# VectorE's maxima and list operations in the order of the text, and two groups of loads issued with later sets of rows

## The chip, the cores and the metric

One core of a Trainium2 chip runs the kernel. The metric is the time of one execution in microseconds on the device; 2252.41 us is the median of three runs before the change. The engines are TensorE (PE in the profile; PEld is its weight load), VectorE (DVE), ScalarE (ACT), GpSimd (POOL) and SyncE (SP), which only issues transfers here.

## The reference

One layer over 256 latent tokens of width 2048: a norm, one projection, an mLSTM and a differential attention side by side, an output projection, and then PEER, a retrieval of experts. The change lies in PEER:

```python
def peer(h, w_pq, sub_keys, expert_u, expert_v):
    q = (h @ w_pq).reshape(B, T, P_HEADS, 2, P_KEY_DIM // 2)
    s = jnp.einsum('bthpd,hpnd->bthpn', q, sub_keys)
    s1, i1 = lax.top_k(s[..., 0, :], P_TOPK)
    s2, i2 = lax.top_k(s[..., 1, :], P_TOPK)
    ...
    idx = jnp.take_along_axis(cand_i, pos, axis=-1)      # expert i1 * 128 + i2
    g = jax.nn.softmax(top_s, axis=-1)
    ...
        act = gelu(jnp.einsum('td,ted->te', hx, expert_u[ix]))
        return jnp.einsum('te,ted->td', gx * act, expert_v[ix])
```

Each token takes 8 heads x 16 of the 16384 experts; each expert is a row of `expert_u` and a row of `expert_v`, 2048 wide. After it, `x + g2 * peer(...)` and a last norm.

## The kernel before

**First product, for all experts.** The kernel multiplies all of `expert_u` with the 256 tokens: 128 blocks of 128 experts, two to a call of `u_pair` (L1229 to L1244) in the loop over `i1`. A block gives one tile `s` in PSUM (two buffers), from two *pieces*. A piece is taken by `take()`, which stages up to three pieces ahead with `stage()`: a 512 KB load `raw` on SyncE's queue (L118), ScalarE's cast to `hi` (L140), and `lo` = raw − hi (L143) on VectorE, or for every fourth piece on POOL. `raw`, `hi` and `lo` have three buffers each. PE then runs eight matmuls with `hi` (512 columns) and eight with `lo` (256 columns). After two pieces VectorE reduces `s` to `act` (L1244), ScalarE applies Gelu (L1713), and `act` goes to a DRAM array (`ag_dram`).

**Beside it, a plan.** After each piece `pump` steps the generator `plan()` 1.15 to 1.7 times (`pace`). It runs, in this order:

- `retrieve`: which experts each token takes, and the softmax.
- `gate_map(t)`, for both halves of the tokens, in two halves each: one-hot matmuls (`g<-o,o`) write the gate of every expert and token to PSUM, ScalarE copies them to `gates`, and `map_out` (L1266 to L1275) then stores a half map by eight transfers of 512 KB on SyncE's queue, in rows of 256 bytes (L1271). Beside each store VectorE takes a maximum over tokens (`most`, L1272), and at the end it copies `gate_tail`.
- `lists()`: from `most`, which experts are used by which groups of tokens (`use`, `many`, `k1`, `kp`, `k2`, `k3`, `single`, `pairs`); `fill` places each kind of expert by matmuls (`g<-pairs,from_on` is the first) and a scan (L1368); `hots` makes one-hot rows (`h`, `at`; L1432, L1433, L1436) whose matmuls `g<-h,h` give the indices of the gathers.
- `soon()`: the second product for the first nine sets of four blocks of rows of `expert_v`. Rows and gates are gathered by indirect transfers on POOL (L1532). The sets are numbered by `n`; the eight rows of sets 0 and 1 are gathered at the start. `resident()` holds eight loads of 256 KB for the end of the kernel: four of `x1` (L1637) and four of `g2` (L1649). `next(loads, None)` issues one with each row of a set, as long as there are any.

The blocks behind that, `v_item`, multiply the rest of `expert_v`.

**What sets the order.** Each engine runs its instructions in the order of its queue. A scheduler orders them ahead of time by its own estimate of times; `tc.keep_in_program_order(i)` holds `i` behind the instruction that the text issued just before it on that engine. Before the change PE's matmuls (`mp_`), the stores, the loads of this phase and the gathers are held so; VectorE's operations are not, until `soon()` begins (`line`).

Of the kernel before, what the change touches and what calls it, by code (L numbers as in the profile page):

```python
# [26 lines left out]
OP = mybir.AluOpType  # L27
AX = mybir.AxisListType
# [59 lines left out]
def build(tc, a, dump=None):  # L88
# [1176 lines left out]
    def map_out(gates, t, hf_):  # L1265
        rows = ag_dram[P:].rearrange("(i p) t -> p i t", p=P)  # L1266
        at = 2 * t * P + 3 * HT * hf_
        w = slice(at, at + HT)
        for i in range(0, P, 16):
            g, j = gates[i // 64], i % 64  # L1270
            tc.keep_in_program_order(nc.sync.dma_start(rows[:, i:i + 16, w], g[:, j:j + 16, :]))  # L1271
            nc.vector.reduce_max(most[:, 4 * t + 2 * hf_:4 * t + 2 * hf_ + 2, i:i + 16].rearrange("p g i -> p i g"),  # L1272
                                 g[:, j:j + 16, :].rearrange("p i (g c) -> p i g c", g=2), axis=AX.X)
            yield
        nc.vector.tensor_copy(gate_tail[:, :, t * P + hf_ * HT:t * P + (hf_ + 1) * HT], gates[1][:, N_LIST - 64:, :])  # L1275
# [32 lines left out]
    def lists():  # L1308
# [4 lines left out]
        nc.vector.memset(one, 1.0)  # L1313
# [4 lines left out]
        nc.vector.tensor_tensor(from_on, from_on, one, op=OP.subtract)  # L1318
        t0 = ls.tile([P, P], F32, name="t0")
        row = ls.tile([P, 1], F32, name="row")  # L1320
        nc.vector.tensor_tensor(t0, ident, iota, op=OP.mult)
        nc.vector.reduce_sum(row, t0, axis=AX.X)
        nc.vector.tensor_scalar(row, row, 1.0, None, op0=OP.add)
        iota4 = ls.tile([P, P, 4], BF16, name="iota4")
        nc.vector.tensor_copy(iota4, b3(iota, 4))
        column = ls.tile([P, N_LIST], BF16, name="column")
        nc.vector.tensor_scalar(column, iota[:, 0:N_LIST], 1.0, None, op0=OP.add)
        yield
        use = ls.tile([P, 8, N_LIST], F32, name="use")
        nc.vector.tensor_scalar(use, most[:, :, 0:N_LIST], 0.0, None, op0=OP.is_gt)  # L1330
        yield
        many = ls.tile([P, 2, N_LIST], F32, name="many")
        for t in range(2):
            nc.vector.reduce_sum(many[:, t], use[:, 4 * t:4 * t + 4].rearrange("p g i -> p i g"), axis=AX.X)
# [4 lines left out]
        nc.vector.memset(zero, 0.0)  # L1339
        nc.vector.tensor_tensor(k1[:, 0], many[:, 0], many[:, 1], op=OP.add)  # L1340
        nc.vector.tensor_scalar(k1, k1, 1.0, None, op0=OP.is_equal)
        yield
        nc.vector.tensor_scalar(k2, many, 1.0, None, op0=OP.is_equal)
        nc.vector.tensor_tensor(kp[:, 0], k2[:, 0], k2[:, 1], op=OP.mult)
        nc.vector.tensor_scalar(k2, many, 0.0, None, op0=OP.is_gt)
        nc.vector.tensor_tensor(k3[:, 0], k2[:, 0], k2[:, 1], op=OP.mult)
        nc.vector.tensor_tensor(k2, k2, k3.to_broadcast([P, 2, N_LIST]), op=OP.subtract)
# [8 lines left out]
        def fill(kind, size, bases):  # L1356
            n, w = kind.shape[1:]
            pre, tot = (psG.tile([P, 4, P], F32, name="g", tag="g").rearrange("p a b -> p (a b)")[:, 0:n * w].rearrange(
                "p (c i) -> p c i", c=n) for _ in range(2))
            rank = ls.tile([P, 4, N_LIST], F32, name="rank", tag="rank", bufs=2)[:, 0:n, 0:w]  # L1360
            pw = put[:, 0:n, 0:w]
            yield
            yield
            mp_(pre, lhsT=from_on, rhs=kind, start=True, stop=True)
            mp_(tot, lhsT=one, rhs=kind, start=True, stop=True)
            yield
            for c in range(n):
                nc.vector.tensor_tensor_scan(rank[:, c], tot[:, c], zero[:, 0:w], 0.0, op0=OP.add, op1=OP.add)  # L1368
            yield
            nc.vector.tensor_tensor(rank, rank, pre, op=OP.add)  # L1370
            nc.vector.scalar_tensor_tensor(pw, rank, float(size * P), kind, op0=OP.is_lt, op1=OP.mult)
            if n == 4:
                nc.vector.tensor_tensor(half_gone[:, :, 0:w], pw[:, 0:2], pw[:, 2:4], op=OP.add)
                pw2 = half_gone[:, :, 0:w]
            else:
                pw2 = pw
            if n == 1:
                nc.vector.tensor_copy(gone[:, 0:w], pw[:, 0])
            else:
# [10 lines left out]
        nc.vector.tensor_tensor(single, use, k1.to_broadcast([P, 8, N_LIST]), op=OP.mult)  # L1390
        nc.vector.tensor_tensor(use[:, 0:4], use[:, 0:4], kp.to_broadcast([P, 4, N_LIST]), op=OP.mult)
        for d in range(4):
            nc.vector.tensor_tensor(pairs[:, 0:4 - d], use[:, 0:4 - d], use[:, 4 + d:], op=OP.mult)
# [20 lines left out]
        nc.vector.tensor_tensor(over, k3[:, 0], gone, op=OP.subtract)  # L1414
# [3 lines left out]
        nc.vector.reduce_sum(zero, places.rearrange("p c i -> p i c"), axis=AX.X)  # L1418
        nc.vector.tensor_scalar(placei[:, 2], zero, float(NOWHERE), None, op0=OP.add)
        nc.vector.tensor_scalar(placei[:, 1], placei[:, 2], P - 1, None, op0=OP.bitwise_and)  # L1420
        nc.vector.tensor_scalar(placei[:, 0], placei[:, 2], 7, None, op0=OP.logical_shift_right)
        nc.vector.tensor_copy(hl, placei[:, 0:2])
# [3 lines left out]
        def hots(i):  # L1426
            i = min(i, N_LIST - 4)
            w = slice(i, i + 4)
            o1 = ls.tile([P, P, 4], BF16, name="h1", tag="h1", bufs=3)
            o2 = ls.tile([P, 4, 2, N_BLOCKS], BF16, name="h2", tag="h2", bufs=3)  # L1430
            at = ls.tile([P, 4, N_BLOCKS], BF16, name="at", tag="at", bufs=2)
            nc.vector.tensor_tensor(o1, hl[:, 1, w].unsqueeze(1).to_broadcast([P, P, 4]), iota4, op=OP.is_equal)  # L1432
            nc.vector.tensor_tensor(at, b3(hl[:, 0, w], N_BLOCKS),  # L1433
                                    iota[:, 0:N_BLOCKS].unsqueeze(1).to_broadcast([P, 4, N_BLOCKS]), op=OP.is_equal)
            nc.scalar.activation(o2[:, :, 0], at, AF.Copy, scale=row)
            nc.vector.tensor_tensor(o2[:, :, 1], at, b3(column[:, w], N_BLOCKS), op=OP.mult)  # L1436
            return o1, o2
# [214 lines left out]
    def soon():  # L1652
# [24 lines left out]
        for n, item in enumerate(work):  # L1677
# [233 lines left out]
```

## Time and profile before

| | us |
|---|---|
| median of three runs | 2252.41 (2245.99 to 2253.37) |
| the profiled execution | 2240.84 |
| its span | 2239.1 |
| PE busy in it | 2146.8 (96%) |
| VectorE busy in it | 1536.1 (69%) |
| ScalarE busy in it | 1022.1 (46%) |
| POOL busy in it | 784.5 (35%) |

The page of the profile shows one execution; times in it count from the start of the span. The first product with its plan fills about 1200 to 2050 us: the maxima of the maps lie between 1347.7 and 1524 us, the lists run from there to about 1755, `soon()` from about 1755 on. A row of the timeline gives the start, the length, the engine, the line, the operation, output<-inputs and shapes, xcount, and in brackets how long the engine had been idle and what ended it. "SPq" rows are SyncE issuing transfers.

### The profile page before, as it was taken

How to read it: one execution, taken by the hardware profiler on the slowest of the kernel's cores; microseconds unless marked ns; L12 is line 12 of the kernel's file. 1: busy time of each engine (PE TensorE's matmuls, PEld its weight loads, DVE VectorE, ACT ScalarE, POOL GpSimd, SP SyncE). 2: the span in 40 equal slices, each digit the busy share in tenths (PEclk: the TensorE clock that was granted, in tenths of full speed). 3: DMA queues.
4: the chain of work that ended last, by engine and by line, in shares of the span. 5: the costliest groups of instructions: out<-in, count | busy, mean ns of one | idle time of the engine just before them, and what ended most of it. 6: DMA issues, size and time to landing. Idle time of an engine off the chain costs nothing. (4 is left out here: it accounts for less than half of the span.)

```text
span 2239.1 us, 37163 instructions
## 1 busy us (share of the span) xinstructions
PE 2146.8 (96%) x14098; PEld 1860.9 (83%) x14098; DVE 1536.1 (69%) x2781; ACT 1022.1 (46%) x1634; POOL 784.5 (35%) x799
## 2 busy tenths in 40 slices
PE   6999999999999999998999999998999999999996
PEld 3668998999899899987998888897888877786773
DVE  3438794566987786855679967777989644544664
ACT  3222232224465854444444678883446333333552
POOL 2122210225554321000223667781221323416763
PEclk9999999999999999999999999999999999999998
DMA  9958883776654678875556568888665798989995
GB/s 379 368 172 310 317 298 96 272 260 195 166 167 131 191 252 279 284 251 179 183 170 193 187 187 236 227 221 235 210 201 183 296 331 332 356 327 380 413 406 226
DMA packets 235845, 563.63 MB, mean 252 GB/s; under 512 B 85218, under 2 KB 118803, under 8 KB 222096
## 3 DMA queue, kind: packets, MB, share of 16 engines
q1 hardware_dynamic: 155328, 339.34, 46.1%
q0 software_dynamic: 45488, 204.33, 25.2%
q10 hardware_dynamic: 34848, 17.57, 2.7%
q8 instruction: 111, 1.82, 0.3%
q14 instruction: 70, 0.57, 0.1%
HBM read 516.99 MB, written 38.93 MB: 248 GB/s over the span
## 5 line engine op out<-in xcount | busy, mean ns | idle before, releaser
L140 ACT CAST hi<-raw 128x1024 fp32r<-128x1024 f32 x528 | 553.2, 1049 | 849.5 <-PE acc L300 275.3
L143 DVE TENSOR_TENSOR lo<-raw,hi 128x1024 fp32r<-128x1024 f32 x476 | 602.4, 1269 | 376.5 <-ACT hi L140 341.3
L94 PE MATMUL s<-h,hi 128*128 128x512 f32 x2048 | 529.1, 400 | 14.5 <-ACT hi L140 13.7
L94 PEld LDWEIGHTS s<-h,hi 128*128 128x128 f32 x2048 | 369.6, 190 | 93.4 <-ACT hi L140 19.3
L300 PE MATMUL acc<-hL,hi 128*128 128x256 f32 x2048 | 333.5, 284 | 0.0
L94 PEld LDWEIGHTS s<-h,lo 128*128 128x128 f32 x2048 | 280.3, 191 | 30.0 <-DVE lo L143 5.5
L300 PEld LDWEIGHTS acc<-hL,hi 128*128 128x128 f32 x2048 | 292.6, 192 | 1.8 <-ACT kA L677 0.3
L94 PE MATMUL s<-h,lo 128*128 128x256 f32 x2048 | 287.1, 283 | 6.9 <-DVE lo L143 3.8
L143 POOL TENSOR_TENSOR lo<-raw,hi 128x1024 fp32r<-128x1024 f32 x52 | 133.6, 2570 | 305.2 <-ACT hi L140 256.7
L300 PE MATMUL acc<-hL,lo 128*128 128x256 f32 x1024 | 175.7, 284 | 0.9 <-DVE lo L143 0.9
L533 DVE SCALAR_TENSOR_TENSOR raw<-raw,cr 128x1024 f32<-128x1024 f32 x128 | 156.3, 1234 | 21.3 <-DMA raw<-w_mod 17.3
L118 POOL DMA_DIRECT2D raw<-w_mod x128 | 67.9, 530 | 289.9 <-DVE raw L533 276.4
L1261 POOL TENSOR_SCALAR o<-iota,i1T,gT 128x128 f32<-128x128 f32 x128 | 147.5, 1160 | 56.4 <-PE g L94 27.9
L1532 POOL DMA_INDIRECT vraw<-expert_v,idxV x96 | 101.5, 1057 | 167.5 <-PE v L94 83.5
L300 PEld LDWEIGHTS acc<-hL,lo 128*128 128x128 f32 x1024 | 150.0, 192 | 2.2 <-DVE lo L143 1.3
L1532 POOL DMA_INDIRECT ag<-ag_dram,idxG x96 | 109.9, 1145 | 79.7 <-DMA ag_dram<-act 37.4
L1561 DVE TENSOR_TENSOR lo<-vraw,hi 128x1024 fp32r<-128x1024 f32 x68 | 82.9, 1225 | 68.4 <-ACT hi L1559 68.2
L300 PE MATMUL acc<-hC,hi 128*128 128x256 f32 x512 | 124.7, 283 | 0.0
L1244 DVE TENSOR_REDUCE act<-s 128x256 f32<-128x512 f32 x126 | 86.1, 684 | 51.0 <-PE s L94 47.4
L94 PE MATMUL v<-hi,l 128*128 128x512 f32 x416 | 114.5, 397 | 0.1
L1559 ACT CAST hi<-vraw 128x1024 fp32r<-128x1024 f32 x68 | 70.8, 1049 | 79.7 <-PE v L94 62.7
L300 PEld LDWEIGHTS acc<-hC,hi 128*128 128x128 f32 x512 | 98.3, 192 | 0.0
(440 smaller groups left out, 3313.4 us busy)
## 6 DMA issues: line engine op xcount, KB each, us to landing
raw<-expert_u SPq DMA_DIRECT2D x256, 512.0 KB, 4.2
raw<-w_in SPq DMA_DIRECT2D x176, 512.0 KB, 4.5
raw<-w_mod POOLq DMA_DIRECT2D x128, 512.0 KB, 5.5
raw<-w_mod SPq DMA_DIRECT2D x64, 512.0 KB, 8.6
raw<-w_out SPq DMA_DIRECT2D x32, 512.0 KB, 4.3
raw<-w_pq SPq DMA_DIRECT2D x32, 512.0 KB, 3.4
ag_dram<-gates SPq DMA_DIRECT2D x32, 512.0 KB, 6.2
ag_dram<-act ACTq DMA_DIRECT2D x126, 128.0 KB, 4.6
```

Source lines behind the costliest of these rows:

```text
L94: tc.keep_in_program_order(mm(*args, **kw))
L118: d = queue.dma_start(r, src)
L140: nc.scalar.copy(h, r)
L143: (nc.vector if shared[0] else nc.gpsimd).tensor_tensor(l, r, h.bitcast(F32), op=OP.subtract)
L300: mm(acc[c][:, g * T:(g + 1) * T], lhsT=hl[sb][:, k2 * 512 + c * P:k2 * 512 + (c + 1) * P], rhs=rhs(sa, g, k), start=first and k2 == 0 and ...
L533: product = nc.vector.scalar_tensor_tensor(r, r, 1.0, cr, op0=OP.mult, op1=OP.mult, accum_out=part[:, h, i:i + 1])
L1244: line(nc.vector.reduce_sum(act[:, e], ps.rearrange("p s t -> p t s"), axis=AX.X))
L1261: (nc.gpsimd if i % 2 else nc.vector).tensor_scalar(o2[:, i], iota, cols[:, i:i + 1], factor[:, i:i + 1], op0=OP.is_equal, op1=OP.mult)
L1532: tc.keep_in_program_order(nc.gpsimd.indirect_dma_start(out=out, out_offset=None, in_=src, in_offset=bass.IndirectOffsetOnAxis(ap=idx[:, b ...
L1559: nc.scalar.copy(h, raw)
L1561: nc.vector.tensor_tensor(l, raw, h.bitcast(F32), op=OP.subtract)
```

## The change

A wrapper `vector` holds each VectorE operation that goes through it behind the one before it in the text. `map_out` and all of `lists()` use it (about 60 calls; the remaining ones differ in nothing but that name). In `soon()` the loads are issued only for `n > 1`, so `x1` goes with the rows of the third set and `g2` with those of the fourth.

```diff
+    class InOrder:
+        def __getattr__(self, name):
+            f = getattr(nc.vector, name)
+            return lambda *args, **kw: tc.keep_in_program_order(f(*args, **kw))
+
+    vector = InOrder()
...
             tc.keep_in_program_order(nc.sync.dma_start(rows[:, i:i + 16, w], g[:, j:j + 16, :]))
-            nc.vector.reduce_max(most[:, 4 * t + 2 * hf_:4 * t + 2 * hf_ + 2, i:i + 16].rearrange("p g i -> p i g"),
+            vector.reduce_max(most[:, 4 * t + 2 * hf_:4 * t + 2 * hf_ + 2, i:i + 16].rearrange("p g i -> p i g"),
                                  g[:, j:j + 16, :].rearrange("p i (g c) -> p i g c", g=2), axis=AX.X)
             yield
-        nc.vector.tensor_copy(gate_tail[:, :, t * P + hf_ * HT:t * P + (hf_ + 1) * HT], gates[1][:, N_LIST - 64:, :])
+        vector.tensor_copy(gate_tail[:, :, t * P + hf_ * HT:t * P + (hf_ + 1) * HT], gates[1][:, N_LIST - 64:, :])
...
-        nc.vector.tensor_tensor(single, use, k1.to_broadcast([P, 8, N_LIST]), op=OP.mult)
-        nc.vector.tensor_tensor(use[:, 0:4], use[:, 0:4], kp.to_broadcast([P, 4, N_LIST]), op=OP.mult)
+        vector.tensor_tensor(single, use, k1.to_broadcast([P, 8, N_LIST]), op=OP.mult)
+        vector.tensor_tensor(use[:, 0:4], use[:, 0:4], kp.to_broadcast([P, 4, N_LIST]), op=OP.mult)
         for d in range(4):
-            nc.vector.tensor_tensor(pairs[:, 0:4 - d], use[:, 0:4 - d], use[:, 4 + d:], op=OP.mult)
+            vector.tensor_tensor(pairs[:, 0:4 - d], use[:, 0:4 - d], use[:, 4 + d:], op=OP.mult)
...
             for j, b in enumerate(item):
                 new[j] = (stage_rows(*b) if n > 1 else rows.pop(0)), new[j]
-                next(loads, None)
+                if n > 1:
+                    next(loads, None)
                 yield
```

PE's queue is the same before and after. VectorE's queue at the last map, before: `most` are its maxima, `gate_tail` the copy behind them, `act` and `lo` the first product's own work.

```order
L1244 TENSOR_REDUCE act<-s 128x256
L143 TENSOR_TENSOR lo<-raw,hi 128x1024
L1272 TENSOR_REDUCE most<-gates 128x16x2 x8
L1275 COPY gate_tail<-gates 128x2x64
L1244 TENSOR_REDUCE act<-s 128x256
L143 TENSOR_TENSOR lo<-raw,hi 128x1024
L1330 TENSOR_SCALAR use<-most 128x1008
L1334 TENSOR_REDUCE many<-use 128x126 x2
```

And after, from the row behind the copy of the half map before it (L136 is the wrapper, L150 is L143, L1251 is L1244):

```order
L136 TENSOR_REDUCE most<-gates 128x16x2
L1251 TENSOR_REDUCE act<-s 128x256
L136 TENSOR_REDUCE most<-gates 128x16x2
L150 TENSOR_TENSOR lo<-raw,hi 128x1024
L136 TENSOR_REDUCE most<-gates 128x16x2 x2
L1251 TENSOR_REDUCE act<-s 128x256
L150 TENSOR_TENSOR lo<-raw,hi 128x1024
L136 TENSOR_REDUCE most<-gates 128x16x2
L1251 TENSOR_REDUCE act<-s 128x256
L136 COPY gate_tail<-gates 128x2x64
```

The batch of eight is taken apart; `act` and `lo` stand between the maxima. The last three come behind the rows shown, again with a `lo` between.

VectorE's queue where `pairs` is made for the first list matmul, before; the scan of that matmul's result (`rank`, L1368) comes eight rows below the last one shown:

```order
L1344 TENSOR_TENSOR kp<-k_16173 128x126
L1390 TENSOR_TENSOR single<-use,k_16170 128x1008
L1345 TENSOR_SCALAR k_16173<-many 128x252
L1391 TENSOR_TENSOR use<-use,kp 128x504
L1346 TENSOR_TENSOR k_16172<-k_16173 128x126
L1393 TENSOR_TENSOR pairs<-use 128x504
L1347 TENSOR_TENSOR k_16173<-k_16173,k_16172 128x252
```

And after, up to that scan:

```order
L1251 TENSOR_REDUCE act<-s 128x256
L136 TENSOR_TENSOR single<-use,k_16170 128x1008
L136 TENSOR_TENSOR kp<-k_16173 128x126
L136 TENSOR_SCALAR k_16173<-many 128x252
L136 TENSOR_TENSOR use<-use,kp 128x504
L150 TENSOR_TENSOR lo<-raw,hi 128x1024
L136 TENSOR_TENSOR k_16172<-k_16173 128x126
L136 TENSOR_TENSOR pairs<-use 128x504
L136 TENSOR_TENSOR k_16173<-k_16173,k_16172 128x252
L136 SCALAR_TENSOR_TENSOR rank<-g,zero 128x126 x4
```

Before, six operations of `lo` lay between `pairs` and the scan; now none does, and an `act` and a `lo` stand between the first list operations and `pairs`.

SyncE's queue from the end of the last map's stores to the first load of `g2`, before:

```order
L118 DMA raw<-expert_u 128x1024 x81
L1637 DMA x_18691<-x_dram 128x512
L118 DMA raw<-expert_u 128x1024
L1637 DMA x_18692<-x_dram 128x512
L1637 DMA x_18693<-x_dram 128x512
L118 DMA raw<-expert_u 128x1024
L1637 DMA x1m<-x_dram 128x512
L118 DMA raw<-expert_u 128x1024 x4
L1649 DMA g_0_18860<-g_dram 128x512
```

And after:

```order
L118 DMA raw<-expert_u 128x1024 x94
L1644 DMA x_19051<-x_dram 128x512
L118 DMA raw<-expert_u 128x1024
L1644 DMA x_19052<-x_dram 128x512
L1644 DMA x_19053<-x_dram 128x512
L118 DMA raw<-expert_u 128x1024
L1644 DMA x1m<-x_dram 128x512
L118 DMA raw<-expert_u 128x1024 x6
L1656 DMA g_0_19296<-g_dram 128x512
```

The loads of `x1` stand 13 row loads later and those of `g2` 15; nothing else on this queue moves.

More of the change, by code (lines that the diff above doesn't have):

```diff
@@ L1312, in lists @@
         one = ls.tile([P, P], BF16, name="one")
-        nc.vector.memset(one, 1.0)
+        vector.memset(one, 1.0)
         from_on = ls.tile([P, P], BF16, name="from_on")
@@ L1317, in lists @@
                                 channel_multiplier=-1)
-        nc.vector.tensor_tensor(from_on, from_on, one, op=OP.subtract)
+        vector.tensor_tensor(from_on, from_on, one, op=OP.subtract)
         t0 = ls.tile([P, P], F32, name="t0")
         row = ls.tile([P, 1], F32, name="row")
-        nc.vector.tensor_tensor(t0, ident, iota, op=OP.mult)
-        nc.vector.reduce_sum(row, t0, axis=AX.X)
-        nc.vector.tensor_scalar(row, row, 1.0, None, op0=OP.add)
+        vector.tensor_tensor(t0, ident, iota, op=OP.mult)
+        vector.reduce_sum(row, t0, axis=AX.X)
+        vector.tensor_scalar(row, row, 1.0, None, op0=OP.add)
         iota4 = ls.tile([P, P, 4], BF16, name="iota4")
-        nc.vector.tensor_copy(iota4, b3(iota, 4))
+        vector.tensor_copy(iota4, b3(iota, 4))
         column = ls.tile([P, N_LIST], BF16, name="column")
-        nc.vector.tensor_scalar(column, iota[:, 0:N_LIST], 1.0, None, op0=OP.add)
+        vector.tensor_scalar(column, iota[:, 0:N_LIST], 1.0, None, op0=OP.add)
         yield
         use = ls.tile([P, 8, N_LIST], F32, name="use")
-        nc.vector.tensor_scalar(use, most[:, :, 0:N_LIST], 0.0, None, op0=OP.is_gt)
+        vector.tensor_scalar(use, most[:, :, 0:N_LIST], 0.0, None, op0=OP.is_gt)
         yield
@@ L1333, in lists @@
         for t in range(2):
-            nc.vector.reduce_sum(many[:, t], use[:, 4 * t:4 * t + 4].rearrange("p g i -> p i g"), axis=AX.X)
+            vector.reduce_sum(many[:, t], use[:, 4 * t:4 * t + 4].rearrange("p g i -> p i g"), axis=AX.X)
         k1, kp = (ls.tile([P, 1, N_LIST], F32, name=n) for n in ("k1", "kp"))
@@ L1338, in lists @@
         zero = ls.tile([P, N_LIST], F32, name="zero")
-        nc.vector.memset(zero, 0.0)
-        nc.vector.tensor_tensor(k1[:, 0], many[:, 0], many[:, 1], op=OP.add)
-        nc.vector.tensor_scalar(k1, k1, 1.0, None, op0=OP.is_equal)
+        vector.memset(zero, 0.0)
+        vector.tensor_tensor(k1[:, 0], many[:, 0], many[:, 1], op=OP.add)
+        vector.tensor_scalar(k1, k1, 1.0, None, op0=OP.is_equal)
         yield
[L1343 to L1347, printed above, removed]
+        vector.tensor_scalar(k2, many, 1.0, None, op0=OP.is_equal)
+        vector.tensor_tensor(kp[:, 0], k2[:, 0], k2[:, 1], op=OP.mult)
+        vector.tensor_scalar(k2, many, 0.0, None, op0=OP.is_gt)
+        vector.tensor_tensor(k3[:, 0], k2[:, 0], k2[:, 1], op=OP.mult)
+        vector.tensor_tensor(k2, k2, k3.to_broadcast([P, 2, N_LIST]), op=OP.subtract)
         yield
@@ L1367, in fill @@
             for c in range(n):
-                nc.vector.tensor_tensor_scan(rank[:, c], tot[:, c], zero[:, 0:w], 0.0, op0=OP.add, op1=OP.add)
+                vector.tensor_tensor_scan(rank[:, c], tot[:, c], zero[:, 0:w], 0.0, op0=OP.add, op1=OP.add)
             yield
-            nc.vector.tensor_tensor(rank, rank, pre, op=OP.add)
-            nc.vector.scalar_tensor_tensor(pw, rank, float(size * P), kind, op0=OP.is_lt, op1=OP.mult)
+            vector.tensor_tensor(rank, rank, pre, op=OP.add)
+            vector.scalar_tensor_tensor(pw, rank, float(size * P), kind, op0=OP.is_lt, op1=OP.mult)
             if n == 4:
-                nc.vector.tensor_tensor(half_gone[:, :, 0:w], pw[:, 0:2], pw[:, 2:4], op=OP.add)
+                vector.tensor_tensor(half_gone[:, :, 0:w], pw[:, 0:2], pw[:, 2:4], op=OP.add)
                 pw2 = half_gone[:, :, 0:w]
@@ L1377, in fill @@
             if n == 1:
-                nc.vector.tensor_copy(gone[:, 0:w], pw[:, 0])
+                vector.tensor_copy(gone[:, 0:w], pw[:, 0])
             else:
-                nc.vector.tensor_tensor(gone[:, 0:w], pw2[:, 0], pw2[:, 1], op=OP.add)
+                vector.tensor_tensor(gone[:, 0:w], pw2[:, 0], pw2[:, 1], op=OP.add)
             yield
             for c, base in enumerate(bases):
-                nc.vector.scalar_tensor_tensor(rank[:, c], rank[:, c], float(base * P - NOWHERE), pw[:, c],
+                vector.scalar_tensor_tensor(rank[:, c], rank[:, c], float(base * P - NOWHERE), pw[:, c],
                                                op0=OP.add, op1=OP.mult)
-            nc.vector.tensor_tensor(places[:, 0:n, 0:w], places[:, 0:n, 0:w], rank, op=OP.add)
+            vector.tensor_tensor(places[:, 0:n, 0:w], places[:, 0:n, 0:w], rank, op=OP.add)
             yield
@@ L1389, in lists @@
         single = ls.tile([P, 8, N_LIST], BF16, name="single")
-        nc.vector.tensor_tensor(single, use, k1.to_broadcast([P, 8, N_LIST]), op=OP.mult)
-        nc.vector.tensor_tensor(use[:, 0:4], use[:, 0:4], kp.to_broadcast([P, 4, N_LIST]), op=OP.mult)
+        vector.tensor_tensor(single, use, k1.to_broadcast([P, 8, N_LIST]), op=OP.mult)
+        vector.tensor_tensor(use[:, 0:4], use[:, 0:4], kp.to_broadcast([P, 4, N_LIST]), op=OP.mult)
         for d in range(4):
-            nc.vector.tensor_tensor(pairs[:, 0:4 - d], use[:, 0:4 - d], use[:, 4 + d:], op=OP.mult)
+            vector.tensor_tensor(pairs[:, 0:4 - d], use[:, 0:4 - d], use[:, 4 + d:], op=OP.mult)
             if d:
-                nc.vector.tensor_tensor(pairs[:, 4 - d:], use[:, 4 - d:4], use[:, 4:4 + d], op=OP.mult)
+                vector.tensor_tensor(pairs[:, 4 - d:], use[:, 4 - d:4], use[:, 4:4 + d], op=OP.mult)
             yield from fill(pairs, 1, [BASE[PAIR + 4 * d + c] for c in range(4)])
-            nc.vector.tensor_tensor(k3[:, 0], k3[:, 0], gone, op=OP.subtract)
+            vector.tensor_tensor(k3[:, 0], k3[:, 0], gone, op=OP.subtract)
         for t in range(2):
@@ L1413, in lists @@
         over = ls.tile([P, N_LIST], F32, name="over")
-        nc.vector.tensor_tensor(over, k3[:, 0], gone, op=OP.subtract)
+        vector.tensor_tensor(over, k3[:, 0], gone, op=OP.subtract)
         nc.gpsimd.dma_start(over_dram, over)
@@ L1417, in lists @@
         hl = ls.tile([P, 2, N_LIST], BF16, name="hl")
[L1418 to L1422, printed above, removed]
+        vector.reduce_sum(zero, places.rearrange("p c i -> p i c"), axis=AX.X)
+        vector.tensor_scalar(placei[:, 2], zero, float(NOWHERE), None, op0=OP.add)
+        vector.tensor_scalar(placei[:, 1], placei[:, 2], P - 1, None, op0=OP.bitwise_and)
+        vector.tensor_scalar(placei[:, 0], placei[:, 2], 7, None, op0=OP.logical_shift_right)
+        vector.tensor_copy(hl, placei[:, 0:2])
         yield
@@ L1454, in lists @@
         mp_(left, lhsT=ones, rhs=over, start=True, stop=True)
-        nc.vector.reduce_sum(t0[:, 0:1], left, axis=AX.X)
-        nc.vector.tensor_copy(n_over, t0[:, 0:1])
+        vector.reduce_sum(t0[:, 0:1], left, axis=AX.X)
+        vector.tensor_copy(n_over, t0[:, 0:1])
         e, at = (ls.tile([P, N_BLOCKS], F32, name=n) for n in ("e", "e_at"))
-        nc.vector.tensor_copy(at, sums[:, 0])
-        nc.vector.scalar_tensor_tensor(e, sums[:, 1], float(P), at, op0=OP.mult, op1=OP.add)
-        nc.vector.tensor_scalar(at, e, -1.0, float(P - 1), op0=OP.add, op1=OP.max)
+        vector.tensor_copy(at, sums[:, 0])
+        vector.scalar_tensor_tensor(e, sums[:, 1], float(P), at, op0=OP.mult, op1=OP.add)
+        vector.tensor_scalar(at, e, -1.0, float(P - 1), op0=OP.add, op1=OP.max)
         for l in range(BOTH):
             w = slice(BASE[l], BASE[l] + CAPS[l])
-            nc.vector.tensor_scalar(at[:, w], at[:, w], 4.0 if l < 8 else 2.0,
+            vector.tensor_scalar(at[:, w], at[:, w], 4.0 if l < 8 else 2.0,
                                     float(2 * TILES[l][0] + group(l, l // 4) // 2 if l < 8 else TILES[l][0]),
                                     op0=OP.mult, op1=OP.add)
-        nc.vector.tensor_copy(idxG, at)
-        nc.vector.tensor_scalar(e, e, float(-P - 1), 0.0, op0=OP.add, op1=OP.max)
-        nc.vector.tensor_copy(idxV, e)
+        vector.tensor_copy(idxG, at)
+        vector.tensor_scalar(e, e, float(-P - 1), 0.0, op0=OP.add, op1=OP.max)
+        vector.tensor_copy(idxV, e)
         ls.release()
```

16 lines of the change are left out of this document (8 added, 8 removed).

## The prediction

> **What bounds the kernel now.** I read the page first, then tables by stretches of time, then the list of waits, then the instructions one by one where TensorE (PE) stood still.
>
> ```profile
> span 2239.1 us, 37163 instructions
> PE 2146.8 (96%) x14098; PEld 1860.9 (83%) x14098; DVE 1536.1 (69%) x2781; ACT 1022.1 (46%) x1634; POOL 784.5 (35%) x799
> ```
>
> PE is busy 2146.8 of 2239.1 us: only its 92 us of idle time can be won, and the change adds no matmul. It touches the stretch from the gate map to the first sets of the second product, 1200 to 2050 us. In these tables the first number is the length, then busy PE, PE's weight loads, VectorE (DVE), ScalarE (ACT), POOL, each with its count, then granted clock, DMA share, GB/s.
>
> ```profile
> 1200.00:2050.00 850.00, 827.05 (x4972) 703.00 (x4971) 605.71 (x995) 448.28 (x734) 364.67 (x272) 0.99 0.78 254
> 1500.00:1550.00 50.00, 42.33 (x240) 35.92 (x239) 32.84 (x42) 20.02 (x33) 11.92 (x9) 0.97 0.85 229
> 1750.00:1800.00 50.00, 43.55 (x246) 37.36 (x246) 22.77 (x39) 15.42 (x16) 21.29 (x20) 1.00 0.90 346
> ```
>
> PE is idle 850.00 − 827.05 = 23 us there: 7.7 while the last map is stored and the lists begin, 6.5 where rows of `expert_v` and the loads for the end run together. What PE waited for in the 850 us (us in total, times, longest):
>
> ```profile
> PE s L94 <- ACT hi L140: 13.7, 12, 3.0
> PE s L94 <- DVE lo L143: 3.8, 4, 1.4
> PE g L94 <- DVE h L1436: 1.4, 1, 1.4
> ```
>
> VectorE is the last named releaser of only 5.2 us. The rest of this is what I charge to the DMA and to the new order.
>
> **The change part by part.** A stall counts twice: after a long one the clock falls.
>
> ```profile
> 1799.36 3.59 PE L94 MATMUL s<-h,hi 128*128 128x512 f32 x8 [2.96 <-ACT hi L140]
> 1803.83 2.00 PE L94 MATMUL s<-h,hi 128*128 128x512 f32 x8
> 1528.71 2.09 PE L94 MATMUL s<-h,hi 128*128 128x512 f32 x8 [1.63 <-ACT hi L140]
> ```
>
> Eight matmuls take 3.59 us after a wait of 2.96, 2.00 undisturbed, 2.09 after a wait of 1.63. I price a stall of about 3 us or more at 3.59 − 2.00 = 1.6 us, once. [...]
>
> *Maxima of the earlier maps.* Eight maxima back to back become single ones between `lo` and `act`. What PE waited for in 1340 to 1510 us:
>
> ```profile
> PE s L94 <- DVE lo L143: 1.2, 2, 0.9
> ```
>
> That is all there is to win: **−1.2** (ends −1.2 and 0).
>
> *Maxima of the last map.* Here the old batch looks guilty of the 7.7 us.
>
> ```profile
> 1514.85 9.10 DVE L1272 TENSOR_REDUCE most<-gates 128x32 f32<-128x1024 f32 x8
> 1522.00:1528.00 6.00, 3.67 (x19) 2.58 (x18) 5.97 (x8) 0.86 (x2) 0.00 (x0) 1.00 1.11 263
> 1528.00:1536.00 8.00, 5.50 (x25) 4.01 (x26) 7.79 (x13) 2.35 (x3) 2.39 (x1) 1.00 1.16 307
> 1536.00:1543.00 7.00, 4.16 (x25) 3.37 (x25) 1.89 (x3) 2.09 (x2) 0.00 (x0) 1.00 1.05 241
> SPq L1271 <- ACT gates L1299: 10.0, 1, 10.0
> L118 SPq DMA_DIRECT2D raw<-expert_u x6: 1887/2576/3077, 1515.2 to 1538.8; - x6
> L118 SPq DMA_DIRECT2D raw<-expert_u x60: 327/328/329, 1559.8 to 1737.9; - x60
> 1542.95 3.27 PE L94 MATMUL s<-h,hi 128*128 128x512 f32 x8 [2.73 <-ACT hi L140]
> ```
>
> But all 16 DMA engines are full (share 1.05 to 1.16) while only 241 to 307 GB/s move: the eight 512 KB stores of the map leave together, once their queue's 10.0 us wait for the gates is over, and the six row loads between them take 2576 ns each to issue instead of 328. In 1536 to 1543, when the batch is long over and VectorE is busy 1.89 of 7 us, PE still loses 2.84 us waiting for `hi`, so for loads. SyncE's order of loads and stores is unchanged. The maxima, spread, free VectorE for data that is not there. **0**; the ends are −(2.33 + 2.50 + 2.84) − 1.6 = −9.3, if the batch was the cause, and +1.6, if the maxima delay a `lo`. I stay at the upper rows because the idle time outlives the batch by 19 us.
>
> *The first step of the lists.* The new order has a price that the old one hid.
>
> ```profile
> 1531.73 1.20 DVE L1390 TENSOR_TENSOR single<-use,k 128x1008 bf16<-128x1008 f32 x1
> 1533.05 0.68 DVE L1391 TENSOR_TENSOR use<-use,kp 128x504 f32<-128x504 f32 x1
> 1533.64 0.22 DVE L1346 TENSOR_TENSOR k<-k 128x126 bf16<-128x126 bf16 x1
> 1533.78 0.68 DVE L1393 TENSOR_TENSOR pairs<-use 128x504 bf16<-128x504 f32 x1
> 1553.00 2.00 PE L94 MATMUL s<-h,hi 128*128 128x512 f32 x8
> 1553.20 0.69 DVE L1244 TENSOR_REDUCE act<-s 128x256 f32<-128x512 f32 x1 [2.02 <-DMA ag_dram<-act]
> 1554.05 1.23 DVE L143 TENSOR_TENSOR lo<-raw,hi 128x1024 fp32r<-128x1024 f32 x1 [0.16 <-ACT hi L140]
> 1555.80 0.39 PE L94 MATMUL g<-pairs,from_on 128*128 128x504 bf16 x1
> 1556.26 2.41 POOL L143 TENSOR_TENSOR lo<-raw,hi 128x1024 fp32r<-128x1024 f32 x1 [7.31 <-ACT hi L140]
> 1557.70 2.06 DVE L143 TENSOR_TENSOR lo<-raw,hi 128x1024 fp32r<-128x1024 f32 x1
> ```
>
> Before, `pairs` was written at 1533.78, some 21 us ahead of the matmul that reads it at 1555.80, and PE's place for that matmul does not move. Now VectorE has, in this order: the `lo` of 1554.05, two operations for `k`, `act`, `single`, `kp`, `k`, `use`, the `lo` of 1557.70, `k`, `pairs`. The first `lo` ends at 1555.28 whatever is done. Two `k` at 0.22 each and `act` at 0.69 bring 1556.4. At 1556.26 POOL has started a `lo`, until 1558.67; beside it the `lo` of 1557.70 took 2.06 instead of 1.23, and ended about one free `lo` after POOL's end. So I start `single` at 1558.67: 1.20, 0.22, 0.22 and 0.68 give 1561.0, `lo` 1562.2, `k` and `pairs` (0.90) 1563.1: **PE waits 1563.1 − 1555.8 = 7.3 us, and loses 1.6 in clock**. Behind that matmul stands all of PE's queue, the next pieces of `s` included; SyncE's loads stop one ring later, which costs nothing more while DMA isn't full. Without POOL's block it is 7.3 − 2.3 = 5.0. The lower end: the `lo` of 1557.70 needs a `hi` whose buffer PE releases only at the end of the eight matmuls of 1553.00, so at 1555.0; `hi` (1.05 by its neighbours), `lo`, `k` and `pairs` then end at 1558.2, a wait of 2.4. Ends +2.4 and +8.9; I take **+8.9**, for the block has its row.
>
> [...]
>
> *Later steps.* The other matmuls of the lists keep their distance to what feeds them, or gain. One gains:
>
> ```profile
> 1670.35 2.73 DVE L1436 TENSOR_TENSOR h<-at,column 128x384 bf16<-128x384 bf16 x1
> 1673.14 0.52 PE L94 MATMUL g<-h,h 128*128 128x192 bf16 x4 [1.38 <-DVE h L1436]
> ```
>
> This product now stands right behind its `at`, ahead of a `lo`, and should be done before PE comes: **−1.4** (ends −1.4 and 0).
>
> *The loads for the end.* 1 MB of `x1` went out beside the rows of sets one and two.
>
> ```profile
> 1783.61 0.38 SPq L1637 DMA_DIRECT2D x<-x_dram  x1
> 1780.00:1790.00 10.00, 7.20 (x40) 5.83 (x39) 3.50 (x4) 3.62 (x4) 2.83 (x3) 1.00 1.02 423
> 1825.00:1840.00 15.00, 15.00 (x86) 13.10 (x86) 6.17 (x10) 4.83 (x5) 8.65 (x8) 1.00 0.98 372
> 1855.00:1870.00 15.00, 15.00 (x88) 13.25 (x87) 7.26 (x11) 4.73 (x5) 7.11 (x8) 1.00 1.01 400
> 1885.00:1900.00 15.00, 14.75 (x89) 11.46 (x89) 6.98 (x11) 5.77 (x6) 0.63 (x1) 1.00 0.92 349
> ```
>
> DMA is full at 1780 (1.02), so 1.05 MB at 0.42 MB/us cost 2.5 us of PE, and without them the last wait, 2.96, falls under the size that costs clock: −2.5 − 1.6 = −4.1. Thirteen row loads later they meet a share of 0.98, then `g2` meets 1.01; PE is busy all of both stretches, so there is cover, and its first loss stands at 1885 (0.25). Bounds 0 and 2.5 + 2.5; I take +1.0, near the rows with no loss. Net **−3.1** (ends −8, if the other waits of the 6.5 go too, and +3).
>
> *Sum.* −1.2 + 0 + 8.9 − 1.4 − 3.1 = +3.2 us on the profiled execution of 2240.84, so 2244.0. That execution lies 5 us under the lowest of the three runs and 11.6 under their median, 2252.41; carried to the median the sum is **2255.6**.
>
> **Rivals.** *A, faster: the batch was the cause.* Then the 9.3 of the store stretch go, `lo` and `pairs` are early, and only the least wait of 2.4 is left: −1.2 − 9.3 + 2.4 − 1.4 − 3.1 = −12.6, so 2239.8. For it: VectorE is busy 5.97 of 6 us in 1522 to 1528. Against it: the share above 1, and 1536 to 1543.
>
> *B, slower: text order starves VectorE while it makes the one-hot rows of the lists (1664 to 1755).*
>
> ```profile
> 1664.00:1710.00 46.00, 44.62 (x284) 39.19 (x283) 45.66 (x75) 26.73 (x36) 9.22 (x5) 1.00 0.59 182
> 1710.00:1755.00 45.00, 45.00 (x290) 39.55 (x289) 42.12 (x62) 25.14 (x33) 8.89 (x4) 1.00 0.59 184
> DVE act L1244 <- PE s L94: 2.1, 2, 1.8
> ```
>
> VectorE has 0.34 + 2.88 = 3.2 us to spare. An `act` that waits for PE holds what stands behind it; two such waits cost 1.05 each. About 15 `act` fall here (one for each 6 us): if all waited so, 15.8 − 3.2 = +12.6 us; half of them, +4.7. Above 3.2 us of waits it is slower, and half gives 2255.6 + 4.7 = 2260.3, all 2268. Against it: the scheduler's `lo` still pass between list operations.
>
> *C, the list wait is hidden* (the matmul is late for another reason): 8.9 less, 2246.7, within no change.
>
> **How the numbers follow.** A measurement of this kernel tells about 0.3% (6.8 us) from no change. The sum as worked out, with its unknowns: 0.50. A: 0.22. B: 0.18. C: 0.10. Faster: A and a little of C, 0.25. Slower: B and the upper end of the sum, 0.21. Same: 0.54. The range takes in A's time at its lower end and half of B's above the upper rows: 2238 to 2264. It leaves out B at its worst and A with the other row waits gone, about 2 in 10.
>
> **What would show it.** PE's wait at the first `g<-pairs` should be 5 to 7 us, released by `pairs`, with a dip of clock behind it. In the store stretch the waits for `hi` should stay near 6 us with the DMA share above 1. The wait of 1.38 for `h` should be gone, the 2.96 near 1799 shorter, and no wait above 1 us new near 1830 to 1870. I am wrong if `pairs` comes early, if the store stretch loses its waits with the batch, or if `g<-h,h` waits repeatedly.

## The result and the profile after

| | before | after | ratio |
|---|---|---|---|
| median, us | 2248.03 (11 runs) | 2263.71 (11 runs) | 1.0064 [1.0048, 1.0079] |
| measured a second time | 2251.4 (21 runs) | 2268.33 (8 runs) | 1.0068 [1.0044, 1.0092] |

The change makes the kernel slower by 0.64% of 2248 us, that is by 14.4 us (the medians themselves lie 15.7 us apart). The first lines of the page after:

```profile
span 2265.3 us, 37135 instructions
...
PE 2157.4 (95%) x14098; PEld 1868.7 (82%) x14098; DVE 1540.9 (68%) x2781; ACT 1023.6 (45%) x1634; POOL 784.4 (35%) x799
```

The two profiled executions are 26 us apart, more than the medians. So the comparison goes by stretches: PE runs the same 14098 matmuls in the same order before and after, and the time between the same two of them tells where it went. Both profiles of the changed kernel are given, and two of the experiments below. Times in us; the first column says where the stretch lies in the profile before.

| stretch | before | after | after, again | order alone | loads alone |
|---|---|---|---|---|---|
| 1394 to 1518: gate map | 123.4 | 122.3 | 122.3 | 122.3 | 123.4 |
| to 1553: the last half map is stored | 35.5 | 35.1 | 37.2 | 36.1 | 36.7 |
| to 1564: first `g<-pairs` | 10.9 | 19.5 | 18.2 | 18.9 | 10.9 |
| to 1686: rest of the placing | 122.1 | 122.0 | 122.6 | 122.6 | 122.3 |
| to 1765: one-hots | 79.1 | 83.6 | 83.0 | 83.6 | 79.1 |
| to 1809: rows of sets one and two | 44.1 | 40.4 | 40.1 | 45.2 | 39.9 |
| to 1991: later sets | 181.5 | 188.0 | 189.5 | 182.0 | 188.8 |
| to 2106: the second product's start | 115.1 | 122.6 | 125.1 | 112.5 | 112.8 |

The first seven rows of the column after differ from before by −1.1 − 0.4 + 8.6 − 0.1 + 4.5 − 3.7 + 6.5 = +14.3 us, close to the measured loss; the second profile of the changed kernel gives +16.3 in the same way. The two halves give +14.1 and +4.5, together more than the whole, so a sum of rows is good to some 2 to 4 us. The last row is taken up under what stays open. Ahead of 1394 us, where the change has moved next to nothing, the profile after is another 5 us longer; those are that execution's own: the kernels that are alike up to that matmul reach it 4 to 5 us apart from one another (1392.4 to 1397.2 us in those without VectorE's new order).

What PE waited for in 1190 to 2060 us after the change (us in total, times, longest):

```profile
PE s L94 <- ACT hi L147: 17.5, 14, 3.7
PE g L94 <- DVE pairs L136: 6.5, 1, 6.5
PE g L94 <- DVE h L136: 4.1, 3, 1.8
PE s L94 <- POOL lo L150: 2.7, 1, 2.7
```

Against before, a wait for `pairs` is new, the waits for `h` are three instead of one (with a fourth for ScalarE's half of `h`, 1.3), the waits for `lo` from VectorE are gone, and those for `hi` have grown from 13.7 to 17.5.

The timeline at the first list matmul, after:

```profile
1557.19 1.22 DVE L150 TENSOR_TENSOR lo<-raw,hi 128x1024 fp32r<-128x1024 f32 x1
...
1558.66 0.68 DVE L1251 TENSOR_REDUCE act<-s 128x256 f32<-128x512 f32 x1
...
1559.26 1.20 DVE L136 TENSOR_TENSOR single<-use,k 128x1008 bf16<-128x1008 f32 x1
1559.75 2.91 POOL L150 TENSOR_TENSOR lo<-raw,hi 128x1024 fp32r<-128x1024 f32 x1 [7.59 <-ACT hi L147]
...
1560.38 2.43 DVE L136 TENSOR_TENSOR kp<-k 128x126 f32<-128x126 bf16 x1
...
1563.05 0.68 DVE L136 TENSOR_TENSOR use<-use,kp 128x504 f32<-128x504 f32 x1
1563.64 1.22 DVE L150 TENSOR_TENSOR lo<-raw,hi 128x1024 fp32r<-128x1024 f32 x1
...
1564.91 0.68 DVE L136 TENSOR_TENSOR pairs<-use 128x504 bf16<-128x504 f32 x1
...
1565.64 0.58 PE L94 MATMUL g<-pairs,from_on 128*128 128x504 bf16 x1 [6.55 <-DVE pairs L136]
...
1566.09 3.90 PE L94 MATMUL s<-h,hi 128*128 128x512 f32 x8
```

VectorE does what the new order says: `lo`, `act`, `single`, `kp`, `use`, another `lo`, `pairs`. PE stands for 6.55 us, and the eight matmuls behind take 3.90 us instead of 2.00. POOL's `lo` holds `kp`: 2.43 us for an operation on 126 columns, which took 0.28 before.

The one-hots, after. Each set of them takes VectorE three operations, `h<-hl,iota`, `at<-hl,iota` and the product `h<-at,column`, and PE's next matmuls read the first and the last:

```profile
1735.46 2.43 POOL L150 TENSOR_TENSOR lo<-raw,hi 128x1024 fp32r<-128x1024 f32 x1 [10.80 <-PE g L94]
1735.55 2.62 DVE L136 TENSOR_TENSOR h<-hl,iota 128x512 bf16<-128x512 bf16 x1
...
1738.09 0.54 DVE L136 TENSOR_TENSOR at<-hl,iota 128x384 bf16<-128x384 bf16 x1
...
1739.16 0.54 DVE L136 TENSOR_TENSOR h<-at,column 128x384 bf16<-128x384 bf16 x1
...
1739.76 0.52 PE L94 MATMUL g<-h,h 128*128 128x192 bf16 x4 [1.17 <-DVE h L136]
```

The first operation takes 2.62 us beside POOL's `lo`, where its like takes 0.42; `at` and the product come late behind it, and PE waits. Beside each POOL `lo` of this stretch one operation of the one-hots lasts 2 us or more, seven times before the change (2.01 to 2.73 us) and seven times after it (2.31 to 2.74). Before, only one of the seven made PE wait: the products were written 3.9 us (median of 32) ahead of the matmuls that read them. After, they are written 1.9 us ahead, and every second one makes PE wait, every 28 us or so.

The loads of `x1` and `g2` now lie between 1837 and 1882 us. That stretch, before and after (length, busy PE, PE's weight loads, VectorE, ScalarE, POOL, each with its count, then granted clock, DMA share, GB/s):

```profile
1840.00:1915.00 75.00, 74.75 (x458) 58.04 (x457) 37.17 (x46) 27.84 (x31) 26.15 (x24) 1.00 0.91 340
```

```profile
1840.00:1915.00 75.00, 69.77 (x412) 54.91 (x414) 32.30 (x43) 25.66 (x29) 24.08 (x22) 0.98 0.93 359
```

And two of PE's waits in it, after:

```profile
1860.15 2.12 PE L94 MATMUL s<-h,hi 128*128 128x512 f32 x8 [1.76 <-ACT hi L147]
1890.43 3.62 PE L94 MATMUL s<-h,hi 128*128 128x512 f32 x8 [2.04 <-ACT hi L147]
```

PE goes from 0.25 us of idle time to 5.23, for `hi`, so for rows that land late (the longest of ScalarE's waits for a row grows from 5.2 to 7.1 us here); the second wait costs clock too: 0.58 was granted from 1890 to 1894.1 us.

### The profile page after: what moved, and what is told of

The parts are those of the page before. It is cut to its first block, busy times and chain, and to the rows that moved or that the text cites. A ratio compares the mean times of both kernels' runs of the same rounds, so it can differ in the third digit from the quotient of the medians.

```text
span 2265.3 us, 37135 instructions
## 1 busy us (share of the span) xinstructions
PE 2157.4 (95%) x14098; PEld 1868.7 (82%) x14098; DVE 1540.9 (68%) x2781; ACT 1023.6 (45%) x1634; POOL 784.4 (35%) x799
## 5 line engine op out<-in xcount | busy, mean ns | idle before, releaser
L150 DVE TENSOR_TENSOR lo<-raw,hi 128x1024 fp32r<-128x1024 f32 x476 | 597.4, 1258 | 372.1 <-ACT hi L147 332.4
L94 PE MATMUL s<-h,hi 128*128 128x512 f32 x2048 | 531.4, 402 | 18.2 <-ACT hi L147 17.5
L150 POOL TENSOR_TENSOR lo<-raw,hi 128x1024 fp32r<-128x1024 f32 x52 | 131.5, 2530 | 314.3 <-ACT hi L147 269.2
L1251 DVE TENSOR_REDUCE act<-s 128x256 f32<-128x512 f32 x126 | 86.4, 686 | 55.9 <-PE s L94 51.5
L94 PEld LDWEIGHTS v<-hi,l 128*128 128x128 f32 x416 | 79.1, 192 | 28.9 <-issue 10.3
```

The source lines that it names most:

```text
L94: tc.keep_in_program_order(mm(*args, **kw))
L150: (nc.vector if shared[0] else nc.gpsimd).tensor_tensor(l, r, h.bitcast(F32), op=OP.subtract)
L1251: line(nc.vector.reduce_sum(act[:, e], ps.rearrange("p s t -> p t s"), axis=AX.X))
```

## The experiments

**The change in halves.** First the loads alone (the kernel before, with the new condition):

```diff
-                next(loads, None)
+                if n > 1:
+                    next(loads, None)
```

> The loads of x1 and g2 with the third and fourth set, VectorE as before. Theory 1 (the slowdown is mainly VectorE's text order: 8.6 us at the first list matmul, some 3 us at the h matmuls; the moved loads give back later about what they win): the waits near 1780 to 1805 shrink from 6.45 us to about 4, with no dip of clock behind them, and PE loses 4 to 7 us more between 1850 and 1915 than before; in sum 0 to +4 us, ratio 1.000 to 1.002. Theory 2 (the moved loads are the main cost): ratio 1.004 or more. Theory 3 (the loads gain as forecast and the rest is loss elsewhere): ratio 0.998 to 0.999.

Ratio 1.0007 [0.9993, 1.0022]. PE's waits for `hi`, first in 1765 to 1806 us, then in 1838 to 1902:

```profile
PE s L94 <- ACT hi L140: 3.8, 5, 0.8
```

```profile
PE s L94 <- ACT hi L140: 7.6, 5, 2.1
```

The first were 6.5 us before, with one of 3.0 among them; the second 0.2. By the stretches the loads win 44.1 − 39.9 = 4.2 us and lose 188.8 − 181.5 = 7.3. Theory 1 holds; the loss is a little over the upper end of what it gave, and the time as a whole does not differ from before within its uncertainty.

Then VectorE's order alone, with the old `next(loads, None)` in the changed kernel:

> VectorE's text order in the maps and lists, the loads as before. Theory 1: PE waits 6 to 7 us at the first g<-pairs with a dip of clock behind it, and four to five times 1.2 to 1.8 us for h; the waits at 1780 to 1805 stay at 6.45 us; in sum +9 to +12 us, ratio 1.004 to 1.0055. Theory 2 (the moved loads are the main cost): ratio below 1.002.

Ratio 1.0057 [1.0040, 1.0075], 12.8 us of 2243. What PE waited for in 1190 to 2060 us:

```profile
PE g L94 <- DVE pairs L136: 6.6, 1, 6.6
PE g L94 <- DVE h L136: 4.1, 3, 1.8
PE g L94 <- ACT h L1442: 1.3, 1, 1.3
```

Nearly all of the slowdown is VectorE's order. The two ratios together give the whole, 1.0064.

**Only the maxima and the tail's copies in text order:**

```diff
-            nc.vector.reduce_max(most[...
+            vector.reduce_max(most[...
-        nc.vector.tensor_copy(gate_tail[...
+        vector.tensor_copy(gate_tail[...
```

> Only the maxima and the copies of the map's tail in text order, the lists and the loads as before. Theory 1: the waits for lo at 1348 to 1415 go (1.2 us), the 7.6 us of the store stretch stay about as large since they are loads that come late; pairs is ready before PE reaches it or nearly so; ratio 0.998 to 1.001. Rival (the batch of maxima holds up the store stretch): its waits fall by more than half and the ratio is 0.997 or less.

Ratio 0.9999 [0.9986, 1.0013]. The gate map takes 122.3 us instead of 123.4; the stretch of the last stores 36.8 instead of 35.5. Taking the batch of maxima apart wins nothing there: the waits for `lo` turn into waits for `hi`. In 1505 to 1556 us, before:

```profile
PE s L94 <- ACT hi L140: 4.5, 3, 2.7
PE s L94 <- DVE lo L143: 2.6, 2, 1.4
```

and with the maxima in order:

```profile
PE s L94 <- ACT hi L147: 6.9, 4, 3.7
...
PE s L94 <- DVE lo L150: 0.9, 2, 0.7
```

**The last stores apart.** The kernel before, its batch of maxima untouched, but the last half map's eight stores go out one by one beside the lists:

```diff
+            if (t, hf_) == (1, 1):
+                late.append((rows[:, i:i + 16, w], g[:, j:j + 16, :]))
...
-        yield from lists()
+        for n, _ in enumerate(lists()):
+            if n % 5 == 2 and late:
+                tc.keep_in_program_order(nc.sync.dma_start(*late.pop(0)))
+            yield
```

> The kernel before, but the eight stores of the last half map are not issued together: each goes out after five steps of the lists, some eight microseconds apart. Theory 1 (the 7.4 us of waits in the store stretch are the DMA's, full with those stores): the waits there fall under 2 us, with no dip of clock, no new ones come beside the lists, and the time falls by 6 to 10 us, ratio 0.9955 to 0.9975. Rival (the batch of eight maxima holds up the stretch): the batch is still there, the waits stay at 5 us or more, ratio 0.999 to 1.001.

Median 2237.03 against 2250.33, ratio 0.9944 [0.9924, 0.9965]. The stretch takes 25.5 us instead of 35.5. Its 50 us, and the loads of rows in 1515 to 1541 (ns: least, median, most):

```profile
1500.00:1550.00 50.00, 48.92 (x297) 43.20 (x296) 36.94 (x48) 26.13 (x44) 17.30 (x11) 1.00 0.77 220
```

```profile
L118 SPq DMA_DIRECT2D raw<-expert_u x7: 327/327/2325, 1517.8 to 1537.9; - x7
```

PE is busy 48.92 us instead of 42.33, a load is issued in 327 ns instead of 2576, and the maxima's batch costs one wait of 1.1 us. The stretch was the stores', and this version beats both kernels, by somewhat more than expected.

**The front of the lists free.** The changed kernel, in which the wrapper holds nothing from the start of `lists()` to the first `pairs`:

```diff
-            return lambda *args, **kw: tc.keep_in_program_order(f(*args, **kw))
+            return lambda *args, **kw: tc.keep_in_program_order(f(*args, **kw)) if held[0] else f(*args, **kw)
```

> As the changed kernel, but VectorE's list operations up to the first pairs are free for the scheduler, which puts pairs two lo operations further ahead of the scan. Theory 1: the wait of 6.55 us at the first g<-pairs falls to 0 to 2 us with no dip of clock behind it, the waits for h stay; 6 to 8.6 us faster than the changed kernel, ratio 1.002 to 1.004 to the kernel before. Rival (the wait at pairs is made up by a later one, DMA being ahead behind it): no faster than the changed kernel, ratio 1.006.

Ratio 1.0049 [1.0030, 1.0068]; the changed kernel stands at 1.0064, in intervals that overlap. The wait at the first `g<-pairs` is gone and its stretch takes 10.9 us, but the next one waits. Its place in the timeline:

```profile
1570.67 2.90 DVE L138 TENSOR_TENSOR pairs<-use 128x378 bf16<-128x378 f32 x2
1570.90 2.53 POOL L152 TENSOR_TENSOR lo<-raw,hi 128x1024 fp32r<-128x1024 f32 x1 [7.82 <-ACT hi L149]
...
1573.62 0.37 PE L94 MATMUL g<-pairs,from_on 128*128 128x504 bf16 x1 [2.35 <-DVE pairs L138]
```

Beside POOL's `lo` of 2.53 us the two `pairs` operations took 2.90. So 8.6 us are won and 126.7 − 122.0 = 4.7 given back. Neither theory had that: the wait moves in part, to the next place where POOL's `lo` meets a product that PE wants.

**The first list matmul later.** VectorE's order of the changed kernel, with six empty steps ahead of the first `fill`:

```diff
+            if d == 0:
+                for _ in range(6):
+                    yield
             yield from fill(pairs, 1, [BASE[PAIR + 4 * d + c] for c in range(4)])
```

> The changed kernel with six empty steps ahead of the first fill, so that PE meets the first g<-pairs about three and a half pieces (10 us) later, while VectorE writes pairs behind the same operations as in the changed kernel. Theory 1 (that matmul waits because PE comes to it too early for the new order): no wait at the first g<-pairs, no dip of clock there, the 60 matmuls around it take 10.9 us instead of 19.5, and nothing is given back in the lists; 6 to 9 us faster than the changed kernel, ratio 1.002 to 1.004 to the kernel before. Rival (VectorE has too much work there and the wait only moves): a wait of 2 us or more at one of the next list matmuls, ratio 1.005 or more.

Ratio 1.0054 [1.0033, 1.0074]. The first matmul no longer waits, the second waits 1.2 us, and a later one 3.65:

```profile
1662.06 2.94 POOL L150 TENSOR_TENSOR lo<-raw,hi 128x1024 fp32r<-128x1024 f32 x1 [8.28 <-ACT hi L147]
1662.73 2.36 DVE L136 TENSOR_TENSOR k<-k,gone 128x126 bf16<-128x126 bf16 x1
...
1665.14 0.28 PE L94 MATMUL g<-k,from_on 128*128 128x252 bf16 x1 [3.65 <-DVE k L136]
```

The single wait behaves as worked out (PE came too early for the new order), but theory 1's second half, that nothing is given back, fails, and the rival's number holds: from the first list matmul to the one-hots PE still idles 4.8 us, against 6.6.

**The one-hots in two more kernels.** Each of the two kernels was executed once, so only the stretches are compared, not the times. One has only the one-hots' operations free again:

```diff
-            vector.tensor_tensor(o1, hl[:, 1, w]...
-            vector.tensor_tensor(at, b3(hl[:, 0, w], N_BLOCKS)...
-            vector.tensor_tensor(o2[:, :, 1], at, ...
+            nc.vector.tensor_tensor(...
```

> The changed kernel, with the one-hot operations of the lists free for the scheduler again. Theory 1 (text order puts the product h beside POOL's lo, which holds it up to 2.3 us): of PE's four waits for h, 5.5 us in all, only one of about 1.4 is left, and the stretch of the one-hots takes 4 us less. Rival (VectorE is full there in any order): the waits stay at 4 us or more.

The stretch takes 79.1 us instead of 83.6, with no wait in it, and the products are written 4.7 us (median) ahead of their matmuls. But the wait at the first of them, in the stretch ahead, grows to 2.3 us, one `g<-h,h` took 364 ns (at most 278 in the changed kernel), and that stretch takes 124.4 us instead of 122.0: of 4.5 us won 2.4 are given back.

The other keeps their order and takes POOL's `lo` away:

```diff
         pace[0] = 1.25
+        on_pool[0] = False
         ready = [hots(0)]
```

> The changed kernel, but from the one-hots of the lists on VectorE makes every lo itself and POOL none. Theory 1 (a POOL lo holds up the product h that PE is about to read): the waits for h of 1.2 to 1.8 us every 28 us go, and no DVE product h takes over 1 us. Rival (VectorE is full there): with one lo in four more on it, some 1.2 us each 11 us, PE's waits for h or lo grow to 8 us or more.

79.1 us too, though VectorE has one `lo` in four more to do, and the products are only 2.5 us (median) ahead; nothing is given back before the stretch (122.2). All 32 first operations and all 32 products, after the change and here (ns):

```profile
L136 DVE TENSOR_TENSOR h<-hl,iota x32: 409/418/2618, 1681.4 to 1767.7; 128x512 bf16<-128x512 bf16 x32
L136 DVE TENSOR_TENSOR h<-at,column x32: 541/556/2625, 1684.2 to 1768.6; 128x384 bf16<-128x384 bf16 x32
```

```profile
L136 DVE TENSOR_TENSOR h<-hl,iota x32: 412/417/420, 1685.0 to 1764.2; 128x512 bf16<-128x512 bf16 x32
L136 DVE TENSOR_TENSOR h<-at,column x32: 545/550/558, 1685.9 to 1766.8; 128x384 bf16<-128x384 bf16 x32
```

No operation of them takes over 558 ns, and no matmul waits for one; 0.7 us remain, for ScalarE's half. POOL's `lo` is the cause, text order the occasion: before, the same collisions mostly fell on operations that PE did not yet need.

**The loads elsewhere.** The kernel before, with `x1` loaded at four steps of the lists and `g2` with the second set:

```diff
+            if n in (50, 55, 60, 65):
+                if not x1_loads:
+                    x1_loads.append(resident())
+                next(x1_loads[0])
...
-                next(loads, None)
+                if n > 0:
+                    next(loads, None)
```

> The kernel before, but x1 is loaded during the lists, where DMA is about 0.6 full, and g2 stays with the second set's rows. Theory 1 (the moved loads win 4.0 us at their old place and lose 6.9 at the new one, because the DMA is full there too): the 4 us are won and nothing is lost, ratio 0.998 to 0.999; the stretch from 1850 to 1915 has no more waits than before. Rival (the gathers' sets run dry in that stretch whatever the loads do): waits of some 7 us stay between 1850 and 1915, ratio 1.000 to 1.002.

Ratio 0.9985 [0.9968, 1.0002]. Sets one and two take 39.8 us instead of 44.1 and the later sets 182.0 instead of 181.5: the gain stays, the loss of the changed kernel is not there, so it belongs to the loads. The time itself stays within its uncertainty.

Both together:

> stores_apart and x1_early together. If both theories hold, the gains add up: 10 to 14 us, ratio 0.994 to 0.996; if the stores and loads get in each other's way beside the lists, new waits of s for hi between 1550 and 1750 and a ratio above 0.997.

Ratio 0.9944 [0.9924, 0.9963], inside the expected range, but no better than the stores alone. Up to 1991 us the 3.7 us of `x1` are there (40.0 and 181.1 against 44.1 and 180.7); behind it the second product takes 3.3 us more (117.8 + 116.3 against 116.2 + 114.6). That stretch with both:

```profile
2020.00:2160.00 140.00, 136.41 (x676) 97.21 (x675) 81.88 (x154) 64.15 (x92) 92.99 (x87) 0.99 0.99 394
```

DMA is full there (0.99); that who comes earlier waits for gathered rows is a guess, which no run isolates.

**The changed kernel once more:**

> The changed kernel once more, for a second profile. If the 9.5 us that PE loses at 2060 to 2130 us in the first one belong to the change, this stretch (600 matmuls) takes about 122 us again; if they are that execution's own, 112 to 118 as in the other kernels. The waits at pairs (6.5 us), for h (5.5 us) and at 1865 to 1920 (some 5 us) should all be there again.

The waits are there again (5.6 us at `pairs`, 4.7 for `h`, 5.6 between 1858 and 1909). The second product's start takes 125.1 us.

## Why the prediction was right and wrong

The forecast was +3.2 us and no measurable change; it is +14.4 us, outside the 6.8 us that the prediction called telling. The measured 2263.71 us lies inside its range by 0.3 us, and that is luck: the range was built on a median before of 2252.41 us, from which its upper end is only 11.6 us away, and the median before of the later runs is 2248.03.

- **Earlier maxima, −1.2.** Right: −1.1 (122.3 against 123.4, in each run with the maxima in order).
- **Last map, 0.** Right, and for the reason given: −0.4 and +1.7 in the two profiles, +1.3 with the maxima alone, and −10.0 when the stores are apart and the batch stays. Rival A falls with it.
- **First step of the lists, 7.3 + 1.6 = +8.9.** Right: 6.55 of wait, +8.6 in sum (+7.3 again). One detail differs: POOL's `lo` started behind `single`, not ahead of it, and held `kp` instead: `single`, first, took its free 1.20 us while POOL's `lo` took 2.91 instead of 2.41, and `kp`, begun at 1560.38, ended at 1562.81, 0.15 us behind POOL's end.
- **Later steps, −1.4.** Wrong in sign: +4.5 us (+3.9 again). The failed step is "The other matmuls of the lists keep their distance to what feeds them, or gain": the products of the one-hots stood 3.9 us ahead of their matmuls before and stand 1.9 us ahead now. The chain of the one-hots was also priced as free of POOL, although the row of 2.73 us stood beside a POOL `lo` of 3.41, as the row of 2.06 stood beside one of 2.41, and that one had been priced in the step before. POOL's `lo` comes with every fourth piece and holds one of these operations in either order, seven times each; with the shorter distance PE waited four times instead of once, which is what the prediction names as a sign of being wrong (`g<-h,h` waits repeatedly). The matmul that was to gain did not: it waited 1.38 us before and waits 1.34 now, for ScalarE's half of `h`. Rival B had the right stretch and by chance the size of its middle case (+4.7), but not the mechanism: without POOL's `lo` the stretch takes 79.1 us, with more work on VectorE.
- **The loads, −4.1 + 1.0.** The gain was right (−3.7, −4.0, and −4.2 alone). The price at the new place was mis-sized: +6.5, +8.0, and +7.3 alone, over its upper end of 5.0. The failed step is "PE is busy all of both stretches, so there is cover". PE was busy there beside a DMA at 0.98 to 1.01, and with the loads alone its waits for `hi` went from 0.2 to 7.6 us: it had no room. 2.1 MB at 0.4 MB/us (400 GB/s at 1855 to 1870) are 5.2 us, by estimate. What the rest is stays open: the changed kernel has a dip of clock there (0.58), but the loads alone have none (1.00 from 1840 to 1895) and lose 7.3.

With 4.5 for −1.4 and −3.7 + 6.5 for −3.1, the prediction's sum becomes +15.0.

**What stays open.** In the stretch from 1991 to 2106 us, whose order the change leaves alone, kernels took 112.5 to 125.1 us. The four that ran one after the other on one chip (the two halves, the maxima alone, the front free) took 112.5 to 113.1, the others, run on other occasions, 115.1 to 125.1; among these the changed kernel and its near variants had 118.9 to 125.1, the rest 115.1 to 117.8. So the occasion has a share in it: the kernel with the front free holds nearly all of both halves of the change and took 113.0. An interaction of both halves is not excluded. The medians need none: the two halves' ratios add up to the whole's, each with an uncertainty of 0.15 to 0.2%.

## What to carry to other kernels

Holding operations in text order decided here also which of them met another engine's instruction that held it up (`kp`, 2.43 us instead of 0.28), and how far ahead of its consumer each was done (1.9 us instead of 3.9): look at what the consumer is about to read, not only at whether the operations fit. PE, busy 15.00 of 15.00 us beside a DMA at 1.01, had no cover for more transfers: the loads there cost 7.3 us, and `x1` moved to a stretch with a share of 0.64 (1550 to 1750 us before) left the later sets within 0.5 us of before. Spreading a burst of stores won 0.56% where rearranging the engine that seemed to be late won nothing. A wait that was taken away came back in part at the next place with the same collision (8.6 us won, 4.7 given back), so take away the collision.

## What the hardware showed that I had not expected

A VectorE operation on 126 columns (`kp`) took 2.43 us beside a POOL `lo` instead of 0.28 before, and one of 0.55 took 2.62; without POOL's `lo` none of 32 was over 0.56. Eight stores of 512 KB in rows of 256 bytes, issued within 24 us with row loads between them, slowed the issue of a row load from 327 to 2576 ns and kept the DMA engines full (share 1.05 to 1.16) at 241 to 307 GB/s, while stretches full of gathers and loads of whole rows moved 423 (1780 to 1790 us before, share 1.02) and 394 (2020 to 2160 with both, 0.99).

The prediction priced a dip of the clock by the length of the wait before it. That length alone did not decide here. In the changed kernel a wait of 2.04 us brought a dip (eight matmuls in 3.62 us, a clock of 0.58 from 1890 to 1894.1 us) and one of 1.76 us none (2.12 us, a clock of 1.00 from 1858 to 1864). But 2.35 us with the front free brought one (seven matmuls in 2.76 us), and 3.65 us with the six empty steps brought none (eight in 2.10). What else decides was not shown.
